# Hybrid block (stick-breaking, forgetting attention, RWKV-7): the RWKV recursion for four pairs of heads per visit, and the first half's matmuls in written order at set distances

## The chip, the cores and the metric

The kernel runs on one core of a Trainium2 chip. The metric is the device time of one execution in microseconds (us); smaller is better. The core's engines are TensorE (PE, with its weight loads shown apart as PEld), VectorE (DVE), ScalarE (ACT), GpSimd (POOL) and SyncE (SP, which issues most DMAs). Each engine executes its own queue of instructions in order; queues wait for each other by semaphores.

## The reference, cut to what matters

One layer of a trunk with T = 256 tokens and D = 2048, all in float32:

```python
u = rms_norm(x)
sb, fox, rw, gates = split(u @ w_in)          # one projection for three branches and three gates
y_a = stick_breaking_attention(sb)            # 4 heads x 128
y_b = forgetting_attention(fox)               # 4 heads x 128
y_c = rwkv7_time_mix(rw)                      # 16 heads x 64
m = sig(g_a) * (y_a @ P_a) + sig(g_b) * (y_b @ P_b) + sig(g_c) * (y_c @ P_c)
x = x + rms_norm(m @ w_out)
x = x + rms_norm(relu(rms_norm(x) @ w_up)^2 @ w_down)
# inside y_c, per head and per token t:
sa = S @ kk_t
S = S * w_t - sa (x) (kk_t * a_t) + v_t (x) k_t
y_t = S @ r_t
y = group_norm(y per head) * ln_w + ln_b + (sum(r * k * r_k)) * v, then times g = sigmoid(gd) @ g_up
```

## The kernel before, in words

All weights stream through the core once, in pieces of 128 x 1024 (`wraw`, line 130). ACT rounds each piece to its high part `whi` (line 140) and DVE takes the rest as `wlo` (line 141); activations are split in the same way (`split`, line 215). A product is then three matmuls, high x high, high x rest and rest x high, so that float32 precision comes from fast passes. In this text a **big** matmul is one of these; it accumulates in a PSUM tile called `gps`. `unit` (line 165) makes 128 columns of the projection with channels on the partitions. `tok` (line 173) makes 512 columns with tokens on the partitions; it is used for the gates (`gate`, line 820) and for the products of the branches (`branch`, line 828).

The first half of the program (lines 233 to 858) is the projection, the three mixers and their gated sum. The second half is the output projection and the MLP, and isn't touched. The mixers (`sb_mix`, `fox_mix`, `rwkv_lora` and `rwkv_half`, lines 340 to 763) are generators. Their matmuls are small ones in full float32, into PSUM tiles called `mps` (four buffers), and they take turns with the big ones: after some big matmuls `gemm` and `tok` call `tick` (line 118), which adds to a credit and advances the generator while there is credit; each `yield` takes some away. I call a run of small matmuls between two big ones a **visit**. The order in which the program is written is a wish only: a scheduler then orders each engine's queue by its own estimate of what is ready first.

`rwkv_half` (line 499) handles eight heads, that is four pairs `PR` of heads (64 channels each, so a pair fills 128 partitions), in four chunks of 64 tokens. It runs twice, and the second run can only begin its recursion late in the first half. Its parts:

- for each pair, decay, keys and their chunk-wise products: lines 544 to 607, the masked products in `SC`;
- centring of v (subtracting the head's mean, by a product with the matrix `cen`), line 613, into partitions 64 to 127 of a tile for each pair, two pairs per visit;
- the inverse of a unit triangular 64 x 64 matrix for each of 8 heads and 4 chunks: DVE solves two 32 x 32 blocks by 62 small operations (lines 632 and 634) and transposes (627, 638, 641), and two visits of 32 matmuls make the third block (647 and 654, each followed by four ACT copies, 650 and 657);
- the recursion over the chunks, lines 667 to 727, in five visits per chunk. Three of them (loop at 673) are staggered over the pairs: state times key and SC times v (680, 685), copied by ACT to `rh` (696), and, for the two pairs before, SC times `rh` (689), copied by DVE into `Xt` (698). Two more (loop at 700), for two pairs each, make the outputs (706, 710, copied by ACT at 726) and the next state (714; ACT scales the old state at 718, DVE adds at 724);
- group norm (742 to 757) and gate product (759 with 128 rows, 760 with 32 rows), for two pairs at a time. Its reciprocal root is `rsqrt` (line 224): a logarithm and an exponential on ACT, each behind a load of the function table, then four DVE operations.

After the projection come, for each of four column groups, two gates and the products of branches a and b (line 839); the generators advance meanwhile. Line 844 then takes all steps of the generators that are left, with no big matmuls between them. Then come, for each of the four groups, the gate of branch c, the product of branch c and the transposes of the sum `m` (line 858).

Of the kernel before, what the change touches and what calls it, by code (L numbers as in the profile page):

```python
# [17 lines left out]
T = 256  # L18
# [3 lines left out]
SHARE = 0.62  # L22
# [27 lines left out]
def hybrid_block(ctx, tc, xt, x, gains, params, consts, lora, gup, wst, out):  # L50
# [42 lines left out]
    done = {}  # L93
# [3 lines left out]
    credit = [0.0]  # L97

    def step():

        if mix[0] is None or fin[0] or (wait[0] is not None and wait[0] not in done):
            return False
        wait[0] = None
# [5 lines left out]
        if isinstance(r, tuple):  # L109
            if r[0] == "need":  # L110
                wait[0] = r[1]
                return True
# [12 lines left out]
    wpos = [0]  # L125

# [3 lines left out]
    def wraw(n=None):  # L130
        raw = wpool.tile([128, HALF], F32, tag="raw", name=nm("raw"), bufs=3)
        nc.sync.dma_start(out=raw, in_=wst[wpos[0] if n is None else n])
        if n is None:
            wpos[0] += 1
# [9 lines left out]
    def wnext():  # L144

        while len(wq) < 1 + AHEAD and wpos[0] < wst.shape[0]:
            wsplit(wraw())
            if side:
                side.pop(0)()
        return wq.pop(0)  # L150

    def gemm(ps, hi, lo, pks, first, last, tick=lambda: None):

        n = len(pks)
        for i in range(n - 1 if last else n):
            PE.matmul(ps, hi[:, i * 128:i * 128 + 128], pks[i], start=first and i == 0, stop=False)  # L156
            if i == 5:
                tick()
        for i in range(n):
            PE.matmul(ps[:, 0:T], lo[:, i * 128:i * 128 + 128], pks[i][:, 0:T], start=False, stop=False)  # L160
        if last:
            PE.matmul(ps, hi[:, (n - 1) * 128:n * 128], pks[n - 1], start=False, stop=True)  # L162
        tick()
# [9 lines left out]
    def tok(pks, lag=1):  # L173
# [6 lines left out]
        def prod(hl, k0, tt):  # L180
            for w, parts in ((hl[0], (0, T)), (hl[1], (0,))):
                for k in (k0, k0 + 1):
                    for part in parts:
                        c = part + tt * 128
                        PE.matmul(ps[tt], pks[k][:, c:c + 128], w[:, (k - k0) * 512:(k - k0) * 512 + 512],  # L185
                                  start=k == 0 and part == 0 and w is hl[0], stop=w is hl[1] and k == n - 1)

        for k0 in range(0, n, 2):
            hl = wnext()
            if k0 >= n - 2 * lag:  # L190
                prod(hl, k0, 0)
                kept.append((hl, k0))
                tick()
                continue
            for w, parts in ((hl[0], (0, T)), (hl[1], (0,))):
                for k in (k0, k0 + 1):
# [5 lines left out]
                    if w is hl[1] or k == k0:  # L202
                        tick(0.7 if w is hl[0] else 0.5)
        yield ps[0]
        for hl, k0 in kept:
            prod(hl, k0, 1)
            tick()
# [25 lines left out]
    p1 = ExitStack()  # L233
    rp = p1.enter_context(tc.tile_pool(name="rp", bufs=1))
    con = rp.tile([128, NCON - 128], F32, name="con")

    def g1(w=T):
        return rp.tile([128, T], F32, tag="g1", name=nm("g1"), bufs=21)
# [25 lines left out]
    xpk = []  # L264

    def xsplit(k):
        if k < 8:
            u = rp.tile([128, 512], F32R, tag="BK", name=nm("xpk"), bufs=8)
        elif k < 13:
            u = rp.tile([128, 512], F32R, tag="AX", name=nm("xpk"), bufs=5)  # L270
# [69 lines left out]
    def sb_mix():  # L340
        yield ("need", "sb")
# [4 lines left out]
        for h in range(4):  # L346
# [4 lines left out]
            yield 0.1  # L351
        for hp in range(2):
# [4 lines left out]
            yield 1.4  # L357
        A.activation(t, t, AF.Ln, bias=1.0)
        for hp in range(2):
# [6 lines left out]
            yield ("stage", 1.8)  # L366
        for hp in range(2):
# [7 lines left out]
            yield 0.6  # L375
# [3 lines left out]
        yield 0.6  # L379
        for hp in range(2):  # L380
# [5 lines left out]
            yield ("stage", 0.2)  # L386
        yield ("stage", 0.1)
        out = []
        for h in range(4):
# [6 lines left out]
            yield 0.35  # L396
        done["ya"] = out

    def fox_mix():
        yield ("need", "fox")  # L400
# [16 lines left out]
        for _ in range(4):  # L417
            yield ("stage", 0.5)
# [14 lines left out]
        yield 0.2  # L433
        for h in range(4):
# [9 lines left out]
            yield 1.2  # L444
# [3 lines left out]
        yield 1.7  # L448
# [4 lines left out]
        yield ("stage", 0.1)  # L453
        V.reciprocal(ri, su)
        for h in range(4):
            V.tensor_scalar(w[:, h, 0:128], w[:, h, 0:128], ri[:, h:h + 1], None, ALU.mult)
            V.tensor_scalar(w[:, h, 128:384], w[:, h, 128:384], ri[:, 4 + h:5 + h], None, ALU.mult)
            yield ("stage" if h == 3 else "go", 0.4)
        for h in range(4):
# [4 lines left out]
            yield ("stage", 0.1)  # L464
        out = []
        for h in range(4):
# [6 lines left out]
            yield ("stage", 0.4)  # L473
# [14 lines left out]
    def rwkv_lora():  # L488
        yield ("need", "lora")
        xl, sy, zz = done["zx"], done["zy"], done["zz"]  # L490
        A.activation(xl[0:64], xl[0:64], AF.Tanh)
        sz = zz[0:32]
        for s in (sy, sz):
            A.activation(s, s, AF.Tanh, scale=0.5)
            V.tensor_scalar(s, s, 0.5, 0.5, ALU.mult, ALU.add)
        done["xl"], done["sy"], done["sz"] = xl, sy, sz
        yield 1.5

    def rwkv_half(hf):
        PR = range(4 * hf, 4 * hf + 4)  # L500
        xl, sy, sz = done["xl"], done["sy"], done["sz"]
# [12 lines left out]
        for i2 in range(2):  # L514
            ss = []
            for p in PR[2 * i2:2 * i2 + 2]:
                yield ("need", f"k{p}")
# [4 lines left out]
            yield ("stage", 0.1)  # L522
# [6 lines left out]
            sq = rp.tile([128, 2, T], F32, tag="AX", name=nm("sq"), bufs=5)  # L529
# [3 lines left out]
            yield 0.6  # L533
            V.tensor_scalar(ri, ri, 1024.0, None, ALU.mult)
            V.tensor_tensor(sc, ri, ri, ALU.mult)
            yield 0.8
# [3 lines left out]
            yield 1.4  # L540
        SC = rp.tile([128, 32, 128], F32, tag="SC", name=nm("SC"), bufs=1)
        At, Bt, Kt, Xt, bon = {}, {}, {}, {}, {}
        ecol = rp.tile([128, 4, 4], F32, tag="ecol", name=nm("ecol"), bufs=2)
        for i, p in enumerate(PR):
# [19 lines left out]
            yield 1.0  # L564
# [6 lines left out]
            At[p] = rp.tile([128, 4, 128], F32, tag="AX", name=nm("At"), bufs=5)  # L571
# [7 lines left out]
            yield 1.9  # L579
# [747 lines left out]
```

## Time and profile before

| | |
|---|---|
| median of three runs | 1570.79 us (1570.1 to 1571.18) |
| span of the profiled execution (first to last instruction) | 1564.8 us |
| median less span: what lies around it | 6.0 us |
| PE busy | 1531.7 us, 98% of the span, 8318 matmuls |
| DVE, ACT busy | 1169.2 us (75%), 913.0 us (58%) |
| DMA | 308.50 MB, mean 197 GB/s |

The profile is one execution. The times of its other views are in us from the span's start. A view by lines groups equal instructions (line of the kernel, engine, operation, output <- inputs by the program's names, shapes, count | busy us, mean ns | idle time just before them and who ended it); a timeline lists instructions in order of time, equal neighbours merged; a view by stretches gives the busy time of each engine, the number of its instructions and the granted PE clock (1.00 is full speed). The profile records a full-float32 matmul as two, a big one as one. Matmuls are pipelined, so one begins long before the last has ended: what a matmul costs is the distance between two starts, not its duration.

### The profile page before, as it was taken

The numbers are of one execution on the slowest core, as the hardware profiler recorded it, in microseconds if no ns is written. First come the engines' busy times: TensorE is split into PE (matmuls) and PEld (weight loads), VectorE is DVE, ScalarE is ACT, GpSimd is POOL, SyncE is SP. The second block draws the span as 40 slices with busy tenths as digits, with TensorE's granted clock in tenths as the row PEclk, the third lists the DMA queues.
The fourth block names the chain that finished last, engine by engine and source line by source line (L and its number), as shares of the span: only waits on it lengthen the run. The fifth ranks groups of instructions, "written<-read, shape, count | busy, mean of one in ns | idle before, by whom it ended". The sixth has DMA issues, their size and how long they took to land.

```text
span 1564.8 us, 22488 instructions
## 1 busy us (share of the span) xinstructions
PE 1531.7 (98%) x8318; PEld 1266.5 (81%) x8318; DVE 1169.2 (75%) x1626; ACT 913.0 (58%) x1392; POOL 82.2 (5%) x152
## 2 busy tenths in 40 slices
PE   7999999999999999999999999999999999999997
PEld 6888888887777877788887888888888787888885
DVE  6875568895577885655555777889988899787855
ACT  7564476555665454644444766667766676566542
POOL 0030001000001000000000000000000000000000
PEclk9999999999999999999999999999999999999998
DMA  7545444453444453455684456888888788787754
GB/s 265 187 139 183 167 150 157 151 179 135 145 154 164 163 176 121 139 188 189 216 315 168 166 189 203 243 245 248 254 258 242 236 237 252 237 259 220 223 192 135
DMA packets 101053, 308.50 MB, mean 197 GB/s; under 512 B 10064, under 2 KB 12496, under 8 KB 100816
## 3 DMA queue, kind: packets, MB, share of 16 engines
q1 hardware_dynamic: 90624, 278.56, 51.9%
q0 software_dynamic: 6912, 25.17, 8.5%
q10 hardware_dynamic: 3408, 3.34, 0.6%
q8 instruction: 65, 1.06, 0.3%
q14 instruction: 44, 0.36, 0.1%
HBM read 279.77 MB, written 2.10 MB: 180 GB/s over the span
## 4 chain that ended last, share of the span: by engine, by line
PE 74%; issue 10%; DMA 7%; DVE 6%; ACT 2%; POOL 1%; POOLq 0%; ACTq 0%; DVEq 0%; SPq 0%
PE gps L200 30%; PE gps L156 15%; PE gps L160 8%; PE gps L185 6%; DMA raw<-raw 4%; DMA raw<-in_wst_dram 3%; DVE wlo L141 3%; PE mps L1094 1%; PE mps L1092 1%; PE mps L1093 1%; ACT whi L140 1%; PE gps L162 1%; PE gps L1094 1%; PE gps L1092 1%; PE gps L1093 1%
## 5 line engine op out<-in xcount | busy, mean ns | idle before, releaser
L141 DVE TENSOR_TENSOR wlo<-raw,whi 128x1024 fp32r<-128x1024 f32 x590 | 716.6, 1223 | 251.2 <-ACT whi L140 231.8
L140 ACT ACTIVATE whi<-raw 128x1024 fp32r<-128x1024 f32 x590 | 618.4, 1055 | 347.6 <-PE gps L200 172.7
L156 PE MATMUL gps<-pk,whi 128*128 128x512 f32 x1495 | 384.3, 395 | 1.1 <-DVE tmp L1015 1.0
L156 PEld LDWEIGHTS gps<-pk,whi 128*128 128x128 f32 x1495 | 277.0, 189 | 58.8 <-issue 4.5
L200 PE MATMUL gps<-whi,pk 128*128 128x512 f32 x1144 | 293.0, 395 | 0.0
L200 PEld LDWEIGHTS gps<-whi,pk 128*128 128x128 f32 x1144 | 212.0, 188 | 46.7 <-issue 2.7
L160 PEld LDWEIGHTS gps<-pk,wlo 128*128 128x128 f32 x1599 | 218.3, 190 | 15.0
L160 PE MATMUL gps<-pk,wlo 128*128 128x256 f32 x1599 | 223.5, 283 | 0.0
L200 PE MATMUL gps<-wlo,pk 128*128 128x512 f32 x572 | 160.9, 396 | 0.0
L200 PEld LDWEIGHTS gps<-wlo,pk 128*128 128x128 f32 x572 | 105.7, 188 | 23.1 <-issue 1.3
L1094 PE MATMUL mps<-wlo,fm 128*128 128x512 f32 x192 | 76.0, 396 | 1.3 <-DVE wlo L141 1.2
L1092 PE MATMUL mps<-whi,fm 128*128 128x512 f32 x192 | 76.3, 397 | 0.8 <-ACT whi L140 0.7
L1014 ACT ACTIVATE tmp<-gps 128x256 f32<-128x256 f32 x64 | 24.5, 383 | 90.0 <-PE gps L162 89.9
L1093 PE MATMUL mps<-whi,fm 128*128 128x512 f32 x192 | 75.1, 391 | 0.0
L185 PE MATMUL gps<-whi,pk 128*128 128x512 f32 x264 | 71.5, 393 | 0.0
L1059 POOL DMA_DIRECT2D raw<-raw x48 | 41.9, 873 | 555.0 <-DVE raw L1056 357.2
L1056 DVE TENSOR_TENSOR raw<-raw,raw 128x1024 f32<-128x1024 f32 x48 | 58.7, 1223 | 1.0
L1094 PE MATMUL gps<-wlo,fm 128*128 128x512 f32 x144 | 57.6, 400 | 1.7 <-DVE wlo L141 1.4
L1092 PE MATMUL gps<-whi,fm 128*128 128x512 f32 x144 | 57.0, 396 | 1.5 <-ACT whi L140 1.4
L185 PEld LDWEIGHTS gps<-whi,pk 128*128 128x128 f32 x264 | 49.1, 188 | 10.6 <-ACT whi L140 0.2
L1093 PE MATMUL gps<-whi,fm 128*128 128x512 f32 x144 | 56.5, 392 | 0.0
L200 PE MATMUL gps<-whi,fm 128*128 128x512 f32 x208 | 51.4, 389 | 0.0
(304 smaller groups left out, 1597.8 us busy)
## 6 DMA issues: line engine op xcount, KB each, us to landing
raw<-in_wst_dram SPq DMA_DIRECT2D x518, 512.0 KB, 4.3
raw<-raw POOLq DMA_DIRECT2D x48, 512.0 KB, 6.5
x<-in_x_dram SPq DMA_DIRECT2D x8, 256.0 KB, 6.4
out_dram<-x SPq DMA_DIRECT2D x8, 256.0 KB, 2.8
x<-in_xt_dram ACTq DMA_DIRECT2D x1, 1024.0 KB, 9.7
fm<-in_gains_dram SPq DMA_DIRECT2D x4, 256.0 KB, 4.4
pk<-in_gains_dram SPq DMA_DIRECT2D x4, 256.0 KB, 4.8
con<-in_consts_dram SPq DMA_DIRECT2D x1, 576.0 KB, 9.3
```

The costliest lines, as they stand in the source:

```text
L140: A.activation(hi, raw, AF.Copy)
L141: V.tensor_tensor(lo, raw, hi.bitcast(F32), ALU.subtract)
L156: PE.matmul(ps, hi[:, i * 128:i * 128 + 128], pks[i], start=first and i == 0, stop=False)
L160: PE.matmul(ps[:, 0:T], lo[:, i * 128:i * 128 + 128], pks[i][:, 0:T], start=False, stop=False)
L185: PE.matmul(ps[tt], pks[k][:, c:c + 128], w[:, (k - k0) * 512:(k - k0) * 512 + 512], start=k == 0 and part == 0 and w is hl[0], stop=w is ...
L200: PE.matmul(ps[tt], pks[k][:, c:c + 128], w[:, (k - k0) * 512:(k - k0) * 512 + 512], start=k == 0 and part == 0 and w is hl[0], stop=False)
L1014: A.activation(b, ps[0][:, T:2 * T], AF.Copy)
L1056: V.tensor_tensor(R[a], R[a], R[b], ALU.add)
L1059: G.dma_start(out=R[a], in_=R[b], accum_op=ALU.add)
L1092: PE.matmul(Q[f], a, w, start=d == 0 and i == 0, stop=False)
L1093: PE.matmul(Q[f], b, w, start=False, stop=False)
L1094: PE.matmul(Q[f], a, wl, start=False, stop=d == 3 and i == 1)
```

## The change

The diff is cut to what the steps speak of; a line of "..." marks what is left out.

- **Order.** The first half is put under a manual schedule for PE alone: PE's queue is now the written order. The other engines' queues are still the scheduler's. `tick` no longer counts credit. It keeps a clock of the big matmuls that were written (0.227 us each, `US`), and a `yield` of a number holds the generator back until that much has passed; a `yield` of a name waits until the named input is written and 2.6 us (`SETTLE`) more.
- **Recursion.** All four pairs go in one visit, three visits per chunk in place of five. Tiles of four pairs (`rhs`, `PB`, `XT`) and one PSUM tile per step replace those of one pair, so ACT and DVE copy more columns by fewer instructions. The state is now added first and scaled after, on DVE alone.
- **Centring.** The product with `cen` goes to column half 0 to 63 for one pair and 64 to 127 for the next, in turn, one visit per half.
- **Gate product.** `zz` and the second part of `gq` are padded with zeros to 128 rows.
- **Gates.** Two gates of branch c are written ahead of the loop that takes the remaining steps, two more between the products of branch c; the order of the weight stream (`order`) follows.

```diff
-            credit[0] -= r[1]
-            return r[0] != "stage"
-        credit[0] -= r
+        if isinstance(r, str):
+            wait[0] = r
+        else:
+            due[0] = clock[0] + r
         return True
-    def tick(f=1.0):
-        credit[0] = min(credit[0] + f * SHARE, 1.5)
-        while credit[0] > 0 and step():
+    def tick(us):
+        clock[0] += us
+        while clock[0] >= due[0] and step():
             pass
...
+    written = ExitStack()
+    written.enter_context(tc.manual_schedule(engines={mybir.EngineType.PE}))
...
-                for cc in range(4):
-                    PE.matmul(ps[64:128, cc * 128:cc * 128 + 128], v[:, cc * 64:cc * 64 + 64], C("cen"),
-                              start=True, stop=True)
+            for cc in range(4):
+                for i, p in enumerate(PR[2 * i2:2 * i2 + 2]):
+                    PE.matmul(ps[HC[i], cc * 128:cc * 128 + 128], done[f"v{p}"][:, cc * 64:cc * 64 + 64], C("cen"),
+                              start=cc == 0, stop=cc == 3)
...
-            yield 0.15 + n * m * 2.1e-3
+            yield 0.6 + n * m * 4e-3
...
+        for c in range(4):
+            ps = mps()
+            if c:
+                for h, hc in enumerate(HC):
+                    for i, p in enumerate(PR):
+                        PE.matmul(ps[hc, 64 * i:64 * i + 64], Bt[p][:, c, 0:64], PB[:, i, hc],
+                                  start=i == 0, stop=False)
+            for i in range(4):
+                for h, hc in enumerate(HC):
+                    PE.matmul(ps[hc, 64 * i:64 * i + 64], SC[64:128, i * 8 + h * 4 + c, 0:64],
+                              XT[i // 2][64:128, i % 2, c, hc], start=c == 0 and i == 0, stop=i == 3)
+            rhs = rp.tile([64, 4, 128], F32, tag="rh", name=nm("rh"), bufs=1)
+            A.activation(rhs[:, :, HC[0]], ps[HC[0], 0:256].rearrange("p (a b) -> p a b", a=4), AF.Copy)
+            V.tensor_copy(rhs[:, :, HC[1]], ps[HC[1], 0:256].rearrange("p (a b) -> p a b", a=4))
+            yield 2.6
+            ps = mps()
+            for i in range(4):
+                for h, hc in enumerate(HC):
+                    PE.matmul(ps[hc, 64 * i:64 * i + 64], SC[0:64, i * 8 + h * 4 + c, 0:64], rhs[:, i, hc],
+                              start=i == 0, stop=i == 3)
+            for d in range(2):
+                A.activation(XT[d][0:64, :, c, HC[0]], duo(ps, HC[0], d), AF.Copy)
+                V.tensor_copy(XT[d][0:64, :, c, HC[1]], duo(ps, HC[1], d))
+            yield 2.8
...
+            if c < 3:
+                for h, hc in enumerate(HC):
+                    s, e = PB[hc, :, hc], ecol[hc, :, c:c + 1].to_broadcast([64, 4, 64])
+                    q = psp[hc, 0:256].rearrange("p (a b) -> p a b", a=4)
+                    if c:
+                        V.tensor_tensor(s, q, s, ALU.add)
+                        V.tensor_tensor(s, s, e, ALU.mult)
+                    else:
+                        V.tensor_tensor(s, q, e, ALU.mult)
+            for i, p in enumerate(PR):
+                A.activation(y[p][:, c * 64:c * 64 + 64], psy[:, 64 * i:64 * i + 64], AF.Copy)
+            yield 3.4
...
-                PE.matmul(ps[:, 0:T], gq[0:32, 1, :], sz, start=False, stop=True)
+                PE.matmul(ps[:, 0:T], gq[:, 1, :], sz, start=False, stop=True)
...
+    thc = [gate(), gate(True)]
     while not fin[0]:
+        due[0] = clock[0]
         step()
...
+    branch(ycp, thc[0], ms[0], False)
+    branch(ycp, thc[1], ms[1], False)
+    thc = [gate(), gate(True)]
+    turn(0)
+    branch(ycp, thc[0], ms[2], False)
+    turn(1)
+    branch(ycp, thc[1], ms[3], False)
+    turn(2)
+    turn(3)
+    written.close()
```

What this does to the queues is seen at three places, all in the second run of `rwkv_half`. In the rows below stand line, operation, output tile <- input tiles, shape of the output and, behind x, how many equal ones follow each other; line numbers of the changed kernel differ from those of before. `whi` and `wlo` are the weights, `pk` activations, and `gps` marks a big matmul.

**First place, PE, where the recursion of the second run begins.** Before, at its second chunk, on PE: four matmuls with the state `Pb` (680) and four with `Xt` (685), two big matmuls, then the next two pairs.

```order
L200 MATMUL gps_5550<-wlo_5751,pk_291 128x512
L680 MATMUL mps_5799<-Pb_5643,Bt_4546 64x64 x2
L680 MATMUL mps_5800<-Pb_5646,Bt_4685 64x64 x2
L685 MATMUL mps_5799<-Xt_5069,SC_4500 64x64 x2
L685 MATMUL mps_5800<-Xt_5076,SC_4500 64x64 x2
L200 MATMUL gps_5549<-wlo_5751,pk_292 128x512
L200 MATMUL gps_5550<-wlo_5751,pk_292 128x512
L680 MATMUL mps_5816<-Pb_5649,Bt_4831 64x64 x2
L680 MATMUL mps_5817<-Pb_5652,Bt_4972 64x64 x2
L685 MATMUL mps_5816<-Xt_5096,SC_4500 64x64 x2
```

Now, on PE, from the last big matmul of the two moved gates (line 187) on: the two visits of the inverse (657, 664), then SC times v (687), SC times `rh` (696), the state (706) and the outputs (710) of the first chunk.

```order
L187 MATMUL gps_5748<-wlo_5878,pk_298 128x512
L657 MATMUL mps_5939<-TW_5935,SC_4869 32x32 x32
L664 MATMUL mps_5976<-SC_4869,TW_5935 32x32 x32
L687 MATMUL mps_6019<-XT_5515,SC_4869 64x64 x4
L687 MATMUL mps_6019<-XT_5527,SC_4869 64x64 x4
L696 MATMUL mps_6031<-rh_6028,SC_4869 64x64 x8
L706 MATMUL mps_6044<-XT_5515,Kt_5009 64x64 x2
L706 MATMUL mps_6044<-XT_5515,Kt_5164 64x64 x2
L706 MATMUL mps_6044<-XT_5527,Kt_5323 64x64 x2
L706 MATMUL mps_6044<-XT_5527,Kt_5470 64x64 x2
L710 MATMUL mps_6045<-SC_4869,XT_5515 64x64 x4
```

The big matmuls between the visits are gone here: the clock of the written order reaches the end of the two gates before the generator has reached the inverse, and the rest is taken by the loop that writes no big matmul. In the first run of `rwkv_half` 12 to 16 big matmuls still stand between two visits.

**Second place, PE, where this stretch ends.** Before, on PE, from the last outputs (710) to the group norm's product (746), the gate products (759, 760) and on to the gate of branch c (gps_6239, gps_6240):

```order
L710 MATMUL mps_6140<-SC_4500,Xt_5103 64x64 x2
L746 MATMUL mps_6155<-gn_6152,con 128x256 x2
L759 MATMUL mps_6171<-zy,gup_6149 128x256
L760 MATMUL mps_6171<-zz,gup_6149 128x256
L759 MATMUL mps_6181<-zy,gup_6168 128x256
L760 MATMUL mps_6181<-zz,gup_6168 128x256
L200 MATMUL gps_6239<-whi_6243,pk_285 128x512 x2
L200 MATMUL gps_6240<-whi_6243,pk_285 128x512 x2
```

Now, on PE, both group norms follow each other, and the next big matmul (line 203) is already the product of branch c, whose inputs pk_6314 and so on are the outputs of the recursion:

```order
L714 MATMUL mps_6227<-Bt_5391,PB_6013 128x64
L746 MATMUL mps_6251<-gn_6248,con 128x256 x2
L759 MATMUL mps_6268<-zy,gup_6244 128x256
L760 MATMUL mps_6268<-zz,gup_6244 128x256
L746 MATMUL mps_6286<-gn_6283,con 128x256 x2
L759 MATMUL mps_6303<-zy,gup_6275 128x256
L760 MATMUL mps_6303<-zz,gup_6275 128x256
L203 MATMUL gps_6338<-whi_5899,pk_6314 128x512 x2
```

All big matmuls of the gate that stood between the two group norms are now ahead of this stretch.

**Third place, DVE, in the recursion of the second run.** Before, on DVE, the copies into `Xt` (698) of the first chunk, four for two pairs, with a weight split (141) between:

```order
L141 TENSOR_TENSOR wlo_5716<-raw_5713,whi_5715 128x1024
L698 COPY Xt_5069<-mps_5678 64x64
L698 COPY Xt_5076<-mps_5678 64x64
L141 TENSOR_TENSOR wlo_5751<-raw_5748,whi_5750 128x1024
L698 COPY Xt_5096<-mps_5704 64x64
L698 COPY Xt_5103<-mps_5704 64x64
```

Now, on DVE, one copy per step of 4 x 64 or 2 x 64 columns (691, 700) and the operations on the state (723 in the first chunk, 720 and 721 in the next); ACT makes the other half of each copy, and each DVE copy waits for the ACT copy of the same tile, as the next ACT copy out of the same PSUM tile waits for the DVE copy before it:

```order
L141 TENSOR_TENSOR wlo_6361<-raw_6358,whi_6360 128x1024
L691 COPY rh_6028<-mps_6019 64x4x64
L700 COPY XT_5515<-mps_6031 64x2x64
L700 COPY XT_5527<-mps_6031 64x2x64
L723 TENSOR_TENSOR PB_6013<-mps_6044,ecol_4870 64x4x64 x2
L691 COPY rh_6085<-mps_6068 64x4x64
L700 COPY XT_5515<-mps_6088 64x2x64
L700 COPY XT_5527<-mps_6088 64x2x64
L720 TENSOR_TENSOR PB_6013<-mps_6101,PB_6013 64x4x64 x2
L721 TENSOR_TENSOR PB_6013<-PB_6013,ecol_4870 64x4x64 x2
```

No weight split stands between these rows any more: there is no big matmul that would use one.

More of the change, by code (lines that the diff above doesn't have):

```diff
@@ L144, in wnext @@
     def wnext():
[L146 to L147 removed]
+        while len(wq) < 1 + AHEAD and (order or wpos[0] < wst.shape[0]):
+            wsplit(wraw(order.pop(0) if order else None))
             if side:
@@ L781, in vtok, with mark @@
         return vs
+    def mark(key, value=True):
+        done[key], at[key] = value, clock[0]
+    g0 = 16 + 8 + 6 + 16 + 8 + 48
+    order.extend(range(wpos[0], g0))
+    for g in range(4):
+        order.extend(range(g0 + 20 * g, g0 + 20 * g + 20))
+    c0 = g0 + 80
+    for g in (0, 2):
+        for i in (0, 8):
+            order.extend(c0 + 12 * (g + j) + k for j in range(2) for k in (range(8) if i == 0 else range(8, 12)))
     for br in ("sb", "fox"):
@@ L851, in hybrid_block, with turn @@
     mpk = []
-    for g in range(4):
-        thc = gate()
-        branch(ycp, thc, ms[g], False)
+    def turn(g):
         for j in range(4):
```

285 lines of the change are left out of this document (129 added, 156 removed).

## The prediction

> **What bounds the kernel now.** I read the page first: span, busy engines, slices.
>
> ```profile
> span 1564.8 us, 22488 instructions
> ...
> PE 1531.7 (98%) x8318; PEld 1266.5 (81%) x8318; DVE 1169.2 (75%) x1626; ACT 913.0 (58%) x1392; POOL 82.2 (5%) x152
> ...
> PE   7999999999999999999999999999999999999997
> ...
> PEclk9999999999999999999999999999999999999998
> ```
>
> PE is busy nearly all the time, in every slice but the first and last, at full clock. So any saving must shorten PE's queue, and any wait that PE now meets is paid in full. Next, the view by stretches, for the second run's recursion and for what follows it in the first half; then the big matmuls alone in the first of them.
>
> ```profile
> 574.90:643.40 68.50, 68.17 (x629) 49.61 (x627) 39.27 (x91) 41.15 (x98) 0.00 (x0) 1.00 0.37 125
> 643.40:770.00 126.60, 126.59 (x569) 103.55 (x569) 74.13 (x85) 59.45 (x73) 0.00 (x0) 1.00 0.54 183
> ```
>
> ```profile
> 574.90:643.40 68.50, 44.48 (x165) 1.00 0.37 125
> ```
>
> The columns are length, busy PE, PEld, DVE, ACT and POOL, clock, DMA share, GB/s. From 574.90 (inverse) to 643.40 (last gate product) PE has no idle time: 165 big matmuls fill the gaps of the recursion. Their distance from start to start is in the timeline behind that stretch:
>
> ```profile
> 645.91 1.07 PE L200 MATMUL gps<-wlo,pk 128*128 128x512 f32 x4
> 646.82 1.98 PE L200 MATMUL gps<-whi,pk 128*128 128x512 f32 x8
> ```
>
> Four take 646.82 - 645.91 = 0.91 us, 0.229 each. So 165 take 37.8 us, and the small matmuls of this stretch cost 68.5 - 37.8 = **30.7 us** of PE time. That is what the recursion's second run costs before.
>
> **The change, part by part.**
>
> *The exposed chain.* In the new queue of PE the second run's inverse, four chunks and both group norms follow each other with no big matmul between. Each step waits for ACT or DVE copies, and these for PE. Its length is built from these rows:
>
> ```profile
> 378.60 0.45 PE L680 MATMUL mps<-Pb,Bt 128*64 128x64 f32 x8
> 378.98 0.45 PE L685 MATMUL mps<-Xt,SC 64*64 64x64 f32 x8
> ...
> 379.42 0.93 ACT L696 ACTIVATE rh<-mps 64x64 f32<-64x64 f32 x4 [1.48 <-PE mps L685]
> ```
>
> ```profile
> 578.59 0.70 PE L654 MATMUL mps<-SC,TW 32*32 32x32 f32 x58 [0.16 <-ACT TW L650]
> 579.64 1.54 ACT L657 ACTIVATE SC<-mps 32x256 f32<-32x256 f32 x4
> ```
>
> ```profile
> 614.67 0.55 PE L706 MATMUL mps<-Bt,Pb 128*128 128x64 f32 x4
> ...
> 615.15 0.34 PE L710 MATMUL mps<-SC,Xt 128*64 128x64 f32 x4
> ```
>
> ```profile
> L696 ACT ACTIVATE rh<-mps 64x64 f32<-64x64 f32 x64 | 12.7, 217 | 8.4 <-PE mps L685 7.3
> L698 DVE COPY Xt<-mps 64x64 f32<-64x64 f32 x64 | 11.4, 217 | 18.1 <-PE mps L689 17.8
> L650 ACT ACTIVATE TW<-mps 32x256 f32<-32x256 f32 x8 | 3.0, 376 | 0.3
> L761 DVE TENSOR_TENSOR g<-mps,g 128x256 f32<-128x256 f32 x8 | 3.2, 419 | 0.2
> ```
>
> - Inverse: 579.64 - 578.59 = 1.05 from the matmuls to ACT, and four copies in 1.54. Two such steps: 5.2 us.
> - Product for `rhs`: eight matmuls (16 records) take from 378.60 to 379.42, 0.8 with the handover to ACT. With the state it is 16 matmuls, of which four can go before the state's last half is done: 1.2. Copies of 256 columns: ACT 0.38 (row 376), DVE 0.42 (row 419), one behind the other: 0.8. Together 2.0; in the first chunk 0.8, since its matmuls go ahead of the inverse's last copies.
> - SC times `rh`: 0.8 for eight matmuls, then four copies of 128 columns in turn on ACT and DVE. A straight line between 217 at 64 columns and 376 or 419 at 256 gives 0.27 and 0.28; with 0.15 of gaps 1.25. Together 2.0.
> - Outputs and state: the L706 row costs 0.24 per matmul with 128 output rows (615.15 - 614.67 = 0.48 for two). I count 2.1 for PE and handover in chunks 2 and 3 and four DVE operations of 0.42 with gaps, 3.9 together; 1.4 in the first chunk (half the matmuls, two operations); 3.5 in the last (1.6 on PE, four ACT copies of 0.22, two operations of the group norm of 0.41, 0.2 of handover).
> - Chunks: (0.8 + 2.0 + 1.4) + 2 x (2.0 + 2.0 + 3.9) + (2.0 + 2.0 + 3.5) = 27.5 us.
>
> For the group norm and what follows the timeline of before is a direct measure:
>
> ```profile
> 628.80 1.13 PE L746 MATMUL mps<-gn,con 128*128 128x256 f32 x4
> ...
> 640.14 1.13 PE L746 MATMUL mps<-gn,con 128*128 128x256 f32 x4
> 641.11 0.60 PE L759 MATMUL mps<-zy,gup 128*128 128x256 f32 x2
> 641.63 0.69 PE L760 MATMUL mps<-zz,gup 32*128 32x256 f32 x2
> 642.26 0.70 PE L759 MATMUL mps<-zy,gup 128*128 128x256 f32 x2
> ...
> 654.44 0.75 DVE L219 TENSOR_TENSOR pk<-g,pk 128x256 fp32r<-128x256 f32 x2
> ```
>
> From the one L746 to the other 11.3 us, less about 1 for a weight split that DVE had between: 10.4. The second L746 and the last gate products: 1.9. So PE can't leave the chain before 5.2 + 27.5 + 10.4 + 1.9 = **45.0 us**. Then the product of branch c needs the last outputs: from the second L746 to the end of the last split (L219) it took 15.0 us, less 1 for a weight split. PE has 1.9 and 36 big matmuls (8.2) to do meanwhile, so it waits some 4 us more: **49 us at full clock**.
>
> *The clock.* On the chain PE works about 14 us of 49 (the matmuls above without handovers), in bits between waits. What the clock does then is seen where the second half begins, in the view by stretches:
>
> ```profile
> 856.65:860.07 3.42, 1.54 (x10) 1.00 0.07 29
> 860.07:863.48 3.41, 3.02 (x11) 0.50 0.01 2
> 863.48:866.89 3.41, 3.04 (x17) 1.00 0.05 11
> ```
>
> One window with PE busy for 1.54 of 3.42 us (45%) was followed by one at clock 0.50; after a full one the clock was 1.00 again. In the chain the share is about 30%, so I take the clock at a half all through, behind a first window at full. Its matmuls then take 14 us more, less 1 for that window: **62 us**. Bounds: 45 (full clock, last 4 us hidden) to 66.
> The Trainium skill, page "TensorE: Matmul & The Clock Gate", section "Part 1: The HAM clock gate (the "warmup" mystery)", says that the clock halves after an idle window of about 3.4 us and is full again after a busy one. No window of the recursion would be wholly idle, so by that rule its matmuls keep full speed up to the group norm (rival B); the row with 45% speaks against reading idle so strictly.
>
> *What the covered part saves* (the first run of the recursion and the rest, between big matmuls):
>
> ```profile
> 290.06 1.96 PE L613 MATMUL mps<-con,g 128*64 128x128 f32 x16
> 291.95 1.67 PE L156 MATMUL gps<-pk,whi 128*128 128x512 f32 x6
> ```
>
> ```profile
> L462 PE MATMUL mps<-ident,foxt 128*128 128x128 f32 x12 | 2.2, 282 | 0.4 <-DVE foxt L456 0.4
> L372 PE MATMUL mps<-sbt,con 128*128 128x128 f32 x8 | 1.7, 300 | 0.7 <-POOL zp L480 0.7
> ```
>
> - Centring: a visit of 1.9 us (290.06 to 291.95), four of them. Two column halves that run side by side halve that: 4 us (bounds 0 to 4).
> - Gate product: the 32-row matmul costs 0.63 (641.63 to 642.26), the 128-row one 0.52. Four in the first run: 0.5 (0 to 1).
> - Fewer visits: outside the exposed stretch 60 stand in the queue for 83. Of these, 20 of the first recursion become 12 and save some 2; merged ones of attention and the transposes 3.5; the idle 0.4 and 0.7 above go if the distances hold, 1. A visit's price isn't in any single row: bounds 0 to 14.
>
> Sum: **11 us** (0 to 19).
>
> *DVE ahead of the chain.* The 32 x 32 solve now has less cover, since it starts when less projection is left: 214 big matmuls (49.0 us) stand between its middle and the inverse, for 240 (55) before.
>
> ```profile
> L634 DVE TENSOR_TENSOR Ti<-Ti,tp 64x31 f32<-64x31 f32 (+15 forms) x62 | 20.6, 333 | 1.5
> L632 DVE TENSOR_TENSOR tp<-U,Ti 64x31 f32<-64x31 f32 (+15 forms) x62 | 20.5, 331 | 1.4
> L641 DVE STREAM_TRANSPOSE SC<-Ti 32x1024 f32<-32x1024 f32 x4 | 8.1, 2014 | 0.0
> L627 DVE STREAM_TRANSPOSE U<-SC 32x1024 f32<-32x1024 f32 x4 | 7.9, 1970 | 0.0
> L638 DVE STREAM_TRANSPOSE TW<-Ti 32x1024 f32<-32x1024 f32 x2 | 4.2, 2119 | 0.0
> ```
>
> ```profile
> L141 DVE TENSOR_TENSOR wlo<-raw,whi 128x1024 fp32r<-128x1024 f32 x590 | 716.6, 1223 | 251.2 <-ACT whi L140 231.8
> ```
>
> One run takes half of these rows: 20.6 + 4.0 + 2.1 + 4.1 = 30.8 us. Fifteen weight splits at 1.22 make 18.3, four operations of the gates 2.7: 52 us against 49. **+3 us** of waiting at the inverse (0 to 6).
>
> *The rest at nothing.* The moved gates' weights come earlier on SP's queue; the DMA share of 0.37 to 0.54 leaves room (0 to 2). The set distances: ACT and DVE copies in the covered visits may land behind a weight piece, and the big matmuls between are to hide that; 0 (0 to 20, rival C). POOL's zeros for padding: POOL is 5% busy, 0.
>
> **Sum** against the profiled execution: 62 - 30.7 - 11 + 3 = +23 us, 1564.8 + 23 = 1588. The median stands 6.0 above the span: **1594 us**.
>
> **The rivals.**
>
> - A, forecast: exposed chain at half clock. 1594, own band 1586 to 1602. For it: the 45% row. Chance 0.50.
> - B: the same chain, but the clock stays full while PE works in bits, with one slow window (+1): 50 - 30.7 - 11 + 3 = +11, **1582**. For it: only one such window stands in the trace, and the end of its idle time may have decided. Chance 0.24. By the rule of the Trainium skill cited above this is what comes.
> - C: the distances are also too short in the covered visits. A copy on ACT, then one on DVE (0.8), each behind one weight piece (DVE 1.22 by the row of L141), is later than the 2.6 us that the written order leaves. PE would wait some 0.45 at each of about 40 visits, 18 more: **1612**. Against it: the queues were met by the same copies before, with PE idle for 1.1 us in all at the two worst lines. Chance 0.12.
> - D, not slower: fewer and larger visits pay to their bound. A PE that changes between full-precision small and big matmuls 23 times less saves 19 instead of 11, the chain runs at full clock with the end hidden (45) and DVE isn't late: 45 - 30.7 - 19 = -5, **1566**. It decides as soon as the covered saving exceeds the exposed chain less 30.7, that is 14 us. Against it: the idle time that could be saved is 1.1 us, and most small matmuls stay. Chance 0.14.
> - That the change doesn't do what it says: its distances are written for a recursion under cover, and the second run has none. That is A and B.
>
> **How the numbers follow.** 0.2% (3.1 us) is about what a measurement of this kernel can tell from no change. D gives faster 0.09, same 0.04, slower 0.01; B's lower edge adds 0.01 to same; A, C and the rest of B are slower: 0.86. The likeliest is A: 1594. The range goes from below B, with its saving at the high end (1582 - 6), to the part of C with 30 visits (1594 + 14): 1576 to 1608. It leaves out D and the upper half of C, 0.2.
>
> **What would show it.** In the new profile: PE below 9 in one or two slices near 580 to 650 us, idle by ACT and DVE releases at the copies of `rhs`, `XT`, `PB` and before L746, some 35 to 45 us in that stretch; PEclk there 5 for A, 9 for B. Idle PE at the copies ahead of 500 us: C. Big matmuls of the first half still at 0.229 each; visits outside the stretch 11 us shorter in sum; PE waits for DVE once at the inverse, 3 us. It is wrong if ACT's and DVE's handovers take less than the rows say once they have no weight pieces to do, or if the scheduler's queues of ACT and DVE hold weight pieces between the copies, which would lengthen the chain by 1 us each.

## The result and the profile after

| | before | changed |
|---|---|---|
| median (4 runs each, one chip) | 1570.44 us (1568.24 to 1571.18) | 1582.13 us (1579.64 to 1586.37) |
| span of the profiled execution | 1564.8 us | 1580.1 us |
| last transposes of `m` (end of the first half) | 770.2 us | 784.7 us |

The change makes the kernel slower: 1.0087 of before, 95% interval 1.0074 to 1.0101. Between the two profiled executions it is 15.3 us, of which 14.5 are in the first half. The changed kernel's profiled execution took 1581.91 us around its span of 1580.1, so 1.8 us lie around a span. One execution further below, of the kernel with the two gates put back, took 3090.92 us; it is left out of that kernel's time, and its profile is read only for who waits for whom.

The page of the changed kernel, busy times and slices of 39.5 us:

```profile
span 1580.1 us, 22365 instructions
...
PE 1530.9 (97%) x8318; PEld 1279.6 (81%) x8318; DVE 1160.4 (73%) x1566; ACT 901.7 (57%) x1340; POOL 85.8 (5%) x155
...
PE   7999999999999999779999999999999999999997
...
PEclk9999999999999999689999999999999999999999
```

Both rows have a dent in the same two slices, 632 to 711 us. The view by stretches, from the inverse (633.40) to the first big matmul behind the last gate product (690.70):

```profile
633.40:690.70 57.30, 39.81 (x466) 33.59 (x465) 15.54 (x36) 20.20 (x55) 0.41 (x2) 0.61 0.11 36
```

57.3 us without a big matmul, 17.5 of them idle, at a mean clock of 0.61. DMA stands nearly still as well (share 0.11): DVE splits no weight piece between 637 and 696 us, so that no weight buffer comes free. The timeline of PE in it shows who is waited for:

```profile
631.43 0.73 PE L187 MATMUL gps<-wlo,pk 128*128 128x512 f32 x2 [0.83 <-DVE wlo L141]
...
633.47 0.75 PE L657 MATMUL mps<-TW,SC 32*32 32x32 f32 x64
636.83 0.24 PE L664 MATMUL mps<-SC,TW 32*32 32x32 f32 x2 [2.60 <-ACT TW L660]
...
638.66 1.07 PE L687 MATMUL mps<-XT,SC 64*64 64x64 f32 x16
640.77 1.57 PE L696 MATMUL mps<-rh,SC 64*64 64x64 f32 x16 [1.03 <-ACT rh L690]
...
654.66 1.57 PE L683 MATMUL mps<-PB,Bt 128*64 128x64 f32 x16 [1.51 <-DVE PB L721]
...
665.65 1.57 PE L683 MATMUL mps<-PB,Bt 128*64 128x64 f32 x16 [1.51 <-DVE PB L721]
...
675.25 2.07 PE L746 MATMUL mps<-gn,con 128*128 128x256 f32 x4 [0.96 <-ACT gn L742]
...
686.51 2.08 PE L746 MATMUL mps<-gn,con 128*128 128x256 f32 x4 [6.22 <-ACT gn L742]
...
690.70 2.20 PE L203 MATMUL gps<-whi,pk 128*128 128x512 f32 x8
```

```profile
700.63 0.96 PE L187 MATMUL gps<-whi,pk 128*128 128x512 f32 x3 [0.85 <-DVE pk L220]
```

One chunk costs 665.65 - 654.66 = 11.0 us. Only one wait follows behind the stretch, 0.85 us for the last outputs.

### The profile page after: what moved, and what is told of

The parts are those of the page before. It is cut to its first block, busy times and chain, and to the rows that moved or that the text cites. A ratio compares the mean times of both kernels' runs of the same rounds, so it can differ in the third digit from the quotient of the medians.

```text
span 1580.1 us, 22365 instructions
## 1 busy us (share of the span) xinstructions
PE 1530.9 (97%) x8318; PEld 1279.6 (81%) x8318; DVE 1160.4 (73%) x1566; ACT 901.7 (57%) x1340; POOL 85.8 (5%) x155
## 4 chain that ended last, share of the span: by engine, by line
PE 72%; issue 11%; DMA 9%; DVE 5%; ACT 2%; POOL 0%; ACTq 0%; POOLq 0%; DVEq 0%; SPq 0%
PE gps L203 29%; PE gps L156 15%; PE gps L160 8%; PE gps L187 6%; DMA raw<-raw 5%; DMA raw<-in_wst_dram 4%; DVE wlo L141 2%; ACT whi L140 1%; PE gps L164 1%; PE mps L1128 1%; PE mps L1130 1%; PE mps L1129 1%; PE gps L1130 1%; PE gps L1128 1%; PE gps L1129 1%
## 5 line engine op out<-in xcount | busy, mean ns | idle before, releaser
L203 PE MATMUL gps<-whi,pk 128*128 128x512 f32 x1144 | 288.8, 392 | 0.0
L203 PE MATMUL gps<-wlo,pk 128*128 128x512 f32 x572 | 155.7, 392 | 0.0
L187 PE MATMUL gps<-whi,pk 128*128 128x512 f32 x264 | 71.8, 393 | 0.9 <-DVE pk L220 0.8
```

## The experiments

Theory E: the loss is the exposed chain of the second run, longer by PE's half clock. Rivals: C, distances too short in the covered visits; N, the four-pair visits are dearer by themselves; and, for the clock, that ACT and DVE set the chain whatever PE's clock. Each ratio is to before on the same chip.

### Shorter distances: the second run gets cover

```diff
-            due[0] = clock[0] + r
+            due[0] = clock[0] + 0.80 * r
```

Only the distances behind a `yield` of a number shrink; the 2.6 us behind a named input stay.

> The changed kernel with every distance of the written order multiplied by 0.8, so that the generator gets ahead: the second run's inverse, all four chunks and most of the group norm then stand between big matmuls (10 to 12 between two visits). Theory E (the loss is the exposed chain: 57.3 us on PE from the inverse to the next big matmul, where the first run's same visits cost 24.3 us between big ones): 33 us less than the changed kernel, 1549 us. Rival C (distances too short in covered visits): at 0.8 the distance behind a product is 2.1 us against the 3.1 that a copy on ACT and one on DVE need behind a weight piece each, so PE waits some 0.4 us at about 40 visits and the second run is no cheaper than it was: 1565 us or more, with idle PE at the copies from 380 us on. Rival N (the four-pair visits themselves are dearer, not their exposure): 1582 us.

Measured: 1550.86 us, ratio **0.9915** (0.9897 to 0.9932), faster than both kernels. The first half ends at 760.7 us, 24.1 earlier than in the changed kernel. The recursion on PE now, with big matmuls between its steps:

```profile
593.89 0.68 PE L687 MATMUL mps<-XT,SC 64*64 64x64 f32 x16
594.51 0.73 PE L203 MATMUL gps<-wlo,pk 128*128 128x512 f32 x2
595.08 1.09 PE L187 MATMUL gps<-whi,pk 128*128 128x512 f32 x4
596.00 0.62 PE L187 MATMUL gps<-wlo,pk 128*128 128x512 f32 x2
596.46 0.61 PE L187 MATMUL gps<-whi,pk 128*128 128x512 f32 x2
597.00 0.68 PE L696 MATMUL mps<-rh,SC 64*64 64x64 f32 x16
```

No wait stands in front of L696. The same stretch, inverse to last gate product, first whole and then its big matmuls alone:

```profile
585.70:664.20 78.50, 77.43 (x696) 61.82 (x695) 39.55 (x58) 41.28 (x76) 0.41 (x2) 1.00 0.44 148
```

```profile
585.70:664.20 78.50, 58.30 (x232) 42.28 (x231) 1.38 (x2) 2.38 (x4) 1.00 0.44 148
```

232 big matmuls at 0.229 are 53.1 us, so the second run costs 25.4 us in place of 57.3 (before: 30.7). Theory E holds, and N falls: covered, the four-pair visits are cheaper than before. Of the 31.9 us saved, 24.1 reach the end of the first half. Some 2.4 come back behind the stretch, where PE waits longer for the last outputs than in the changed kernel and runs slow matmuls after it (rows below). The other 5 come back ahead of the inverse, where the visits stand closer; they were not traced one by one.

```profile
673.63 0.50 PE L187 MATMUL gps<-whi,pk 128*128 128x512 f32 x1 [1.04 <-ACT pk L219]
674.98 1.50 PE L187 MATMUL gps<-whi,pk 128*128 128x512 f32 x3 [0.85 <-DVE pk L220]
```

Not all of the gain is explained. The second half, which no kernel touches, took 787.7 us in this profile and 793 to 797 in the other ten of before, of the changed kernel and of the variants. So of the 16.5 us between this profile and before's, 9.5 lie in the first half and follow from the distances; 7 lie in the second half, and why is open. That 1550.86 comes so near to the 1549 expected is partly luck.

### Shorter still: 0.75 and 0.7

The same line with 0.75 and 0.70.

> The changed kernel with all distances times 0.75. The whole second run, both group norms included, then stands between big matmuls, and 9 to 10 big matmuls behind the last gate product. Against 0.8 the wait of PE for the last outputs (3.5 us ahead of and in the product of branch c) should fall by half. Theory E with nothing else late: ratio 0.989 to 0.991 of before. Rival C (distances now too short): new waits of PE at the copies and for DVE's solve take that back, 0.993 or more.

> The changed kernel with all distances times 0.7. The second run ends with its last gate product some 75 big matmuls ahead of branch c, so no wait for its outputs is left. Theory E: 4 us less than at 0.8, ratio 0.988 to 0.990. Rival C: 1.8 us behind a product for copies of 0.8 us and up to 2.3 us of weight pieces, and DVE's solve (30.8 us of its own in 28 us of distances) is the bound: PE waits at the inverse for 5 us or more in each run, ratio 0.993 to 1.000.

Measured: 1555.95 us, 0.9928 (0.9908 to 0.9948), and 1558.51 us, 0.9950 (0.9932 to 0.9968). The first half ends at 759.6 and at 768.3 us. So 0.75 wins 1 us there over 0.8: no wait for the last outputs is left, but PE waits longer for DVE, 2.1 us at a pair's products (1.3 at 0.8) and 0.9 for a weight split. With the second half as long as in the other profiles (795.7 us), its time lies above that of 0.8; which of the two is better stays open. At 0.7 PE waits for DVE again, as in rival C. Two of these waits on PE's timeline of the 0.7 kernel:

```profile
251.09 2.08 PE L600 MATMUL mps<-Bt,At 64*128 64x128 f32 x16 [3.73 <-DVE At L583]
```

```profile
456.56 0.73 PE L203 MATMUL gps<-wlo,pk 128*128 128x512 f32 x2 [1.30 <-DVE wlo L141]
```

They are waits in the pairs' products (4.4 us in all) and for weight splits around the solve (2.7), more than for the copies of the recursion. At the inverse, where 5 us or more had been expected in each run, PE waits for 1.0 in all. The waits also slow PE: the L600 group that waited takes 2.08 us at half clock. The ten executions of this kernel go from 1553.6 to 1565.22 us and the profiled one took 1564.1, so its waits may be larger than usual.

### Keeping the clock up in the exposed chain

```diff
+    def warm(n):
+        if "keep" in done:
+            ps = gps()
+            for i in range(n):
+                PE.matmul(ps, upk[0][:, 0:128], upk[1], start=True, stop=True)
```

From the loop of remaining steps on it is called behind the first product of the inverse, behind each step of the chunks and once in the group norm; nobody reads the results.

> The changed kernel with big matmuls on activations, whose results nobody reads, in the waits of the exposed chain (3 behind each product, 6 behind the state, 8 in the inverse, 20 in the group norm), so that PE's clock stays up. If the half clock makes a good part of the chain's 57.3 us: granted clock near 1.0 in that stretch, and about 8 us less, 1574 us. If ACT and DVE set the chain and the clock costs next to nothing: 1582 us, or up to 4 us more where an added matmul stands in the way.

> The changed kernel with fewer added matmuls in the chunks (2 behind each product, 4 behind the state) and more in the group norm (36), so that PE idles a little before each step of the chunks and the group norm is covered. Theory clock: granted clock near 1.0 throughout; the chain from the inverse to the product of branch c, 57.3 us in the changed kernel and 52.6 with the denser filling, comes down to my sum at full clock, 45 to 49 us. Theory filling: the dense filling had not delayed anything, or the clock falls again with the idle time, 52 us or more.

Measured: 1579.31 us, 1.0093 (1.0074 to 1.0112) with the dense filling, 1576.51 us, 1.0058 (1.0040 to 1.0076) with the lighter one. The stretch in each, at clocks 0.88 and 0.93:

```profile
634.20:686.90 52.70, 48.55 (x540) 37.25 (x539) 15.49 (x36) 20.94 (x56) 0.41 (x2) 0.88 0.12 39
```

```profile
633.90:683.55 49.65, 46.81 (x540) 35.77 (x539) 15.65 (x36) 19.49 (x54) 0.41 (x2) 0.93 0.13 42
```

The starts of two chunks with the lighter filling, on PE's timeline (L684 there is L683 of the changed kernel):

```profile
655.06 1.04 PE L684 MATMUL mps<-PB,Bt 128*64 128x64 f32 x16 [0.53 <-DVE PB L724]
...
663.16 1.04 PE L684 MATMUL mps<-PB,Bt 128*64 128x64 f32 x16 [0.53 <-DVE PB L724]
```

A chunk takes 8.1 us in place of 11.0, and the stretch 49.7 in place of 57.3: **the clock is 7.7 us of the chain**, and ACT, DVE and PE at full clock make the rest. The dense filling reached 52.7. Its chunks take 8.1 us too (656.46 to 664.55 on its timeline), so the added matmuls did not delay them, against what I had thought. Most of the difference lies at the end: with its group norm filled by 20 in place of 36, the last L746 and gate products run at half clock and take 4.9 us in place of 2.4. The first half ends at 780.7 and 779.9 us, 4 and 5 us earlier. In the lighter one 2.4 of the missing gain are behind the stretch, in waits for the last outputs (0.75 and 0.85 us) and half clock after them. The 8 us that were expected of the dense filling didn't come: its ratio shows no gain, and 4 us in one profile aren't resolved in it.

### The two gates put back

```diff
-    thc = [gate(), gate(True)]
     while not fin[0]:
...
+    thc = [gate(), gate(True)]
     branch(ycp, thc[0], ms[0], False)
```

> The changed kernel with the two moved gates put back behind the remaining steps. If the gates serve as cover for DVE's solve of the 32 x 32 blocks (43.6 us of big matmuls, and DVE needs some 31 us plus what its queue holds besides): PE waits for DVE ahead of the inverse for 25 to 30 us, 1607 us or more. If their place doesn't matter, because the generator's chain only begins later or earlier by as much: 1582 us.

Measured: 1606.68 us (median of three), 1.0257 (1.0230 to 1.0285), some 25 us more than the changed kernel. So the moved gates are a needed part of this change. The view of waits (engine, what waits, for whom: us in total, times, longest) puts the wait where it was expected, ahead of the inverse, for DVE's transpose behind the solve (its place counts here, not its length):

```profile
PE mps L657 <- DVE TW L648: 22.4, 1, 22.4
```

### PE's written order ended ahead of the gates

```diff
+    written.close()
     thc = [gate(), gate(True)]
...
-    written.close()
```

> The changed kernel with PE's written order ended ahead of the moved gates; from there on the scheduler orders PE. It puts 48 big matmuls of branch c, for pairs of the first run, between the steps of the chunks, and leaves the group norms exposed. Theory E: each takes 0.229 us of waiting away, 11 us, 1571 us. If the waits are too short or too late for them, or the visits grow by being broken up: 1578 to 1582 us.

Measured: 1575.52 us, 1.0061 (1.0036 to 1.0086); the first half ends at 780.7 us, 4.1 earlier. The stretch from the inverse to the last gate product, now with 48 big matmuls in it:

```profile
633.20:696.20 63.00, 51.31 (x513) 37.94 (x513) 20.00 (x40) 25.01 (x60) 0.41 (x2) 0.76 0.20 66
```

63.0 less 48 at 0.229 (11.0) is 52.0, so the steps cost 5.3 us less than in the changed kernel, half of what the added cover is long, and the time lies between the two that were expected. The other half was paid, by steps that came later or by big matmuls at half clock (mean clock 0.76 here); how it divides was not separated. Elsewhere in the first half PE's order is that of the changed kernel, matmul for matmul. Ahead of the gates both kernels follow the written order, so this run can't tell what it does there; from the gates on it differs from the scheduler's in this stretch alone, and costs 4 us.

### The changed kernel again

> The changed kernel once more, beside the other three on one chip: 1.0087 of before as measured, within its interval. A ratio of 1.005 or less would mean that the first result was one of its chip.

Measured beside the centring and the two shortest distances: 1580.86 us, 1.0094 (1.0071 to 1.0117). The first result stands.

### Centring halves alone, in the kernel before

```diff
-            for p in PR[2 * i2:2 * i2 + 2]:
-                ps = mps()
-                for cc in range(4):
-                    PE.matmul(ps[64:128, cc * 128:cc * 128 + 128], v[:, cc * 64:cc * 64 + 64], C("cen"),
-                              start=True, stop=True)
+            ps = mps()
+            for cc in range(4):
+                for i, p in enumerate(PR[2 * i2:2 * i2 + 2]):
+                    PE.matmul(ps[64 * i:64 * i + 64, cc * 128:cc * 128 + 128], done[f"v{p}"][:, cc * 64:cc * 64 + 64],
+                              C("cen"), start=cc == 0, stop=cc == 3)
```

> The kernel before with one part of the change alone: the centring product of two pairs goes to column halves 0 to 63 and 64 to 127 in turn, into one PSUM tile. If the halves work side by side, as the changed kernel's visits of 1.99 us for 32 records (1.98 us for 16 before) say: the four visits of 1.98 become four of about 1.0, 4 us less, ratio 0.9975, with the end of the first half earlier by 4 us. If they don't, or if the saved time comes back as a later wait: 1.000 within its interval, and the first half ends as before.

Measured: 1578.09 us, **1.0071** (1.0050 to 1.0092): slower. My expectation was wrong, and not by the halves. The visit on PE's timeline:

```profile
290.54 1.09 PE L612 MATMUL mps<-con,g 128*64 128x128 f32 x16
291.57 1.67 PE L156 MATMUL gps<-pk,whi 128*128 128x512 f32 x6
```

1.03 us from start to start in place of 1.89. Yet the first half ends at 777.9 us, 7.7 later. PE now reaches its weights before DVE has finished the solve (the transposes of line 641) and turned to the split:

```profile
341.85 1.92 DVE L641 STREAM_TRANSPOSE SC<-Ti 32x1024 f32<-32x1024 f32 x1
343.81 3.50 DVE L141 TENSOR_TENSOR wlo<-raw,whi 128x1024 fp32r<-128x1024 f32 x3
```

```profile
345.09 1.42 PE L200 MATMUL gps<-wlo,pk 128*128 128x512 f32 x4 [2.83 <-DVE wlo L141]
346.30 3.38 PE L200 MATMUL gps<-whi,pk 128*128 128x512 f32 x8
```

A wait of 2.83 us, and behind it eight big matmuls that take 3.38 us in place of 1.98, at half clock. In the second run PE waits 1.78 us for ACT's copy of the inverse, and big matmuls at half clock follow here too. Held against before big matmul by big matmul, PE loses 6.0 us around the first inverse and 4.7 around the second, three times the 3.5 that the halves save. These 3.5 were not there to be had: in the first run DVE was still at its solve, in the second ACT's copy came late, and the clock made the waits cost more than their length.

### Halves with more distance in the solve

```diff
-            yield 0.15 + n * m * 2.1e-3
+            yield 0.23 + n * m * 2.1e-3
```

> The kernel before with the centring halves alone, as in the run of that name, and a little more distance in the 32 x 32 solve (0.23 for 0.15 per step), so that 306 and 270 big matmuls stand between centring and inverse for 280 and 240. If the halves alone came out slower because DVE's solve was late by what PE had saved (2.99 us of waiting for a weight split at 341.7 us, 1.0 and 1.84 at the inverse, and slow matmuls behind): these waits go, the first half ends 3 to 4 us earlier than before's 770 us, ratio 0.996 to 0.999. If the halves themselves are the harm (their copies out of two partition halves, or one PSUM tile for two pairs): as slow as the halves alone, 1.005 to 1.009.

Measured: 1572.88 us, 1.0034 (1.0021 to 1.0046), half of the loss gone; the first half ends at 776.3 us. The wait for the weight split at 345 us is gone, as expected, but the forecast of a gain fails, and the time lies between the two expectations. PE still waits for ACT's copy at the first inverse:

```profile
355.23 0.24 PE L654 MATMUL mps<-SC,TW 32*32 32x32 f32 x2 [2.17 <-ACT TW L650]
```

And the generator ends later, so that the second run's steps have fewer big matmuls among them and the clock falls there:

```profile
600.00:650.00 50.00, 49.99 (x382) 36.15 (x379) 27.79 (x71) 27.84 (x72) 0.00 (x0) 0.93 0.26 84
```

Held against before in the same way, PE loses some 2 us in the first run and 7 in the second. How much of it is the clock was not separated, nor is it shown that the halves do no harm of their own.

## Why the prediction was right, and which terms were mis-sized

The sign, the mechanism and the range were right; the forecast of 1594 lies 12 us above the median, and rival B gave 1582 for another reason. By its steps:

- **The exposed chain.** Right in kind: no cover, copies of 0.268 to 0.424 us for the 0.27 to 0.42 taken, one behind the other. At full clock 45.0 was worked out up to the last gate product; the lighter filling, with the clock at half in its first part, shows 49.7. One part doesn't follow from its rows: for the second L746 and the last gate products 1.9 stood, where the rows of before give 3.3 (640.14 to 643.40) and the lighter filling took 2.4.
- **The clock.** Right in kind, and B wrong in kind: it was at half through most of the chain. It is worth 7.7 us or a little more, where 13 stood in the sum (49 to 62). The wait for the last outputs was taken too large as well, 4 us for the 1.1 lost there, since at half clock PE needs 4.2 us for the last L746 and gate products (686.51 to 690.70), while the outputs get ready. The chain of 57.3 with this 1.1 makes 58.4, where 62 stood: longer than counted at full clock, with a smaller price of the clock and a smaller wait.
- **The saving of the covered part.** 11 stood in the sum, some 14 came: the first half is 14.5 longer, the second run 57.3 - 30.7 = 26.6 longer, and about 1 each stands for the split at 631 us and for the outputs at 700 us, so all else is 14 shorter. Where it comes from is seen in the distances from start to start on PE, line by line, ahead of the second inverse. Centring gives 3.8, for the 4 counted. The gate products give 1.9 for the 0.5 counted: a pair of them takes 0.68 us now (462.47 to 463.15, rows below the list), for 1.15 in the rows of before. The recursion gives 0.9, attention some 1, the pairs' products 0.2. Some 4 lie in the big matmuls beside the visits, whose distances exceed 0.229 by less now.
- **DVE ahead of the chain.** 3 taken at the inverse; 0.83 measured, at a weight split before it.
- **What lies around the span.** I added 6.0 us from before's median and profile. It is 1.8: the profiled execution of before was some 4 us shorter than the median of its runs. This is 4 of the 12 us. Chain with clock, saving, DVE and span are all off to the same side, so that these errors add up.

The gate products of one pair in the first run, now:

```profile
462.47 0.59 PE L759 MATMUL mps<-zy,gup 128*128 128x256 f32 x2
462.90 0.59 PE L760 MATMUL mps<-zz,gup 128*128 128x256 f32 x2
463.15 1.74 PE L203 MATMUL gps<-whi,pk 128*128 128x512 f32 x6
```

So B's number was met by the wrong way: B had the clock full and a saving of 11, the runs show it at half and a saving of 14. Rival C doesn't occur at the distances of this change; at 0.7 of them PE waits for DVE, though less at the copies than the rival had it. Rival D falls: its point was a saving above the chain less 30.7, here 27.7 us, and 14 came. Idle PE in the stretch was 17.5 us, not the 35 to 45 that I named. The half clock fills a part of the waits with slower matmuls, but PE's own work was also taken too small: 14 us, where the covered second run of the 0.8 kernel costs 25.4 at full clock.

The chances gave the clock's two cases 0.50 and 0.24 by one row of 45%. It pointed the right way, and that was partly luck: the last section shows that the busy share alone doesn't decide.

## What to carry to other kernels

Before trusting a static order, look in it for steps that depend on each other with nothing between: their cost is their whole latency, here 57 us for work that costs 25 when it is covered, and distances shorter by 20 to 25% turned a loss of 0.9% into a gain of 0.7 to 0.85%, of which 0.6 to 0.7 is explained. Distances have two limits: too long, and the chain runs out of cover at the end; too short, and the engine behind the chain (DVE's solve here) is late. Time saved on the busiest engine is worth nothing where the next engine has no slack, as the halves showed; and a wait on PE can cost more than its length, when the clock falls behind it (2.83 us of waiting, then 1.4 more in the next eight matmuls).

## What the runs showed of the hardware that was not expected

The clock doesn't need an idle window to fall. In the changed kernel's chain, in windows of 3.41 us that begin where the clock changed:

```profile
635.34:638.75 3.41, 1.45 (x66) 1.08 (x68) 1.23 (x1) 2.54 (x7) 0.00 (x0) 1.00 0.77 259
638.75:642.17 3.42, 2.39 (x32) 2.01 (x32) 0.42 (x1) 1.88 (x5) 0.00 (x0) 0.50 0.32 125
642.17:645.58 3.41, 3.05 (x43) 2.80 (x43) 1.43 (x4) 0.89 (x6) 0.00 (x0) 0.50 0.00 0
645.58:648.99 3.41, 2.38 (x46) 1.85 (x43) 0.68 (x2) 0.88 (x4) 0.00 (x0) 1.00 0.02 5
648.99:652.41 3.42, 3.42 (x38) 3.17 (x36) 0.33 (x2) 0.27 (x1) 0.00 (x0) 0.50 0.00 0
652.41:655.82 3.41, 1.90 (x19) 1.74 (x19) 1.68 (x4) 0.57 (x4) 0.00 (x0) 0.50 0.00 0
```

A window with PE busy for 2.38 of 3.41 us (70%) at full clock is followed by one at half. One with 3.05 (89%) at half is followed by one at full, but a later one with 3.42 of 3.42 (648.99) is not. Nor does it take any idle time at all: in the 0.8 kernel a window at full clock with PE busy throughout is followed by one at half.

```profile
183.65:187.06 3.41, 3.41 (x20) 2.80 (x20) 0.17 (x1) 1.25 (x3) 0.00 (x0) 1.00 0.57 189
187.06:190.48 3.42, 3.42 (x11) 2.74 (x10) 2.05 (x3) 1.87 (x4) 0.10 (x1) 0.50 0.00 0
```

So busy time in the profile alone doesn't decide; whether the size of the matmuls or how the records of pipelined ones overlap is the reason was not tested. The Trainium skill, page "TensorE: Matmul & The Clock Gate", section "Part 1: The HAM clock gate (the "warmup" mystery)", gives an idle window of about 3.4 us as the condition for half clock; the length of the windows agrees with the trace, the condition doesn't.
